# Output blocks turned on VectorE, one product and one load reordered, last forms subtracted earlier: a hybrid encoder layer on one core

## The chip, the cores and the metric

The kernel runs on one core of one Trainium2 chip. The metric is the device time of one launch in microseconds (us). The engines are TensorE (PE, with its weight loads as PEld), VectorE (DVE), ScalarE (ACT), GpSimd (POOL) and SyncE (SP), which issues most of the DMA transfers. Each engine runs its own queue of instructions in order; semaphores make one wait for another.

## The reference

One layer, for 512 prompt frames and 64 sample frames (576 columns together). All data are float32.

```python
hn = rmsnorm(x, g_norm1)
q, k, v, gb, gc, hc = split(hn @ w_in)             # 8 heads x 128 each; 1024 conv channels each
q, k = rmsnorm(q, g_q), rmsnorm(k, g_k)            # per head
o_attn = stick_breaking(q, [k_past, k], [v_past, v])   # strictly causal; the sample has 512 cached frames
u = gc * hc
o_conv = gb * (conv_w[0]*u[t-2] + conv_w[1]*u[t-1] + conv_w[2]*u[t])
x = x + concat(rmsnorm(o_attn, g_attn_out), rmsnorm(o_conv, g_conv_out)) @ w_out
h2 = rmsnorm(x, g_norm2)
x = x + (silu(h2 @ w_gate) * (h2 @ w_up)) @ w_down     # D_MODEL 2048, D_FF 5632
```

Outputs are the new x of prompt and sample, the new keys and values, and the convolution's state.

## The kernel before, in words

Activations lie with channels on the 128 partitions and the 576 frames along the free axis, in two halves of 288. A float32 product is made of three matmuls of a rounded format (fp32r): a number is split into a rounded high part and the rest, and high x high, low x high and high x low are added in PSUM. The splits cost a ScalarE cast (L228, the high part) and a VectorE subtraction (L229, the rest).

The big weight products are done by a seven-product scheme (Strassen-Winograd) on 2 x 2 blocks: two neighbouring channel tiles of the input, two of the output, two halves of the frames. One *unit* is a pair of output tiles (256 output channels) over `m` pairs of input tiles. It has seven products, numbered 1 to 7; each is `m` x 3 matmuls (`multiply`, L405) and its weights are one of seven sums of the unit's four weight blocks, made by VectorE in `weight_sums` (four additions, L345 to L353) and split into a tile `whl` by `prepare`. There are four `whl` buffers, and `prepare` runs four products ahead of `run`. The products land in three kinds of PSUM tiles: `psy` and `psv` from a rotation of three banks (`ps_pj`), `psx` (bank z0) and `psw` (bank z1 or z2 by the unit's parity). ScalarE copies partial results out (`kept`, L428), VectorE and GpSimd add them up (L445 to L452).

`order` is the hand-written list of (unit, product). It starts with `opening`; from the third unit on it repeats one pattern: the next unit's product 1, this one's 3 and 4, the next one's 2, 6, 7, 5. PE's order is always the program's. The other engines' order is made by the tile framework's scheduler in most phases; from the last unit of the gate and up phase on (`manual`), ScalarE, VectorE, SyncE and GpSimd follow the program too. A `Pipeline` of generators spaces small jobs in *ticks*: one tick is one step of `multiply`, three matmuls, and `yield 9` means nine ticks later.

Phases in order of time: input projection (to about 575 us), attention beside the output projection (to 755), second norm, gate and up (860 to 1830), down (to the end).

*Attention.* `heads` starts a head every 29 ticks; `attend` yields between its steps, with output projection products between them. At its end a head reads the sample's values with `os_` (L1296): four blocks of cached values and `vtok[:, 4]`, weighted by `ws` (an exponential on ScalarE, L1224). Then `fetch_v(h + 1)` loads the next head's values: `vtok[:, :4]` (L1045, the 512 prompt frames), `vtok[:, 4]` (L1046, the last 128 frames, sample included) and the cached `cV` (L1047); `split_v` casts the first three blocks into `hbe` and `vz`.

*Gate and up.* `finish` scales each result by the norm's row `R2`, multiplies gate and up, and `put_forms` makes the seven sums of the hidden activations (forms) for the down phase and writes them to `hid_dram` (`put_form`: cast L228, subtraction L229, DMA L1453). For the last pair `last_forms` does this in spaced steps, in the first products of the down phase.

*Down.* The order of units is the list `DOWN`; eight pairs of output tiles (`d`) are summed in SBUF blocks `acc[d, c, i]` (128 channels x 288 frames). Units 29 to 36 of the list are the last visits of each `d`: as each of their four blocks is finished, `store_y` turns it into rows of frames. Nine ticks later PE transposes the block in three pieces into PSUM (L1612), ScalarE copies it back in two instructions (L1615, L1617), and SyncE stores it (L1603, L1605, L1620), two to four DMAs a block. All 32 blocks go this way, 28 of the first seven units and four of the last, the last unit's with some of the stores on the queues of ScalarE and GpSimd. The next but one unit's weights are loaded by SyncE (L328) when a unit's products 3 and 4 have been split.

The kernel already has another way of turning a tile, in `tokens` (L807 to L815): VectorE transposes 32 x 32 blocks, and stores of 32 partitions with runs of 32 floats put them in place.

Of the kernel before, what the change touches and what calls it, by code (L numbers as in the profile page):

```python
# [10 lines left out]
F32 = mybir.dt.float32  # L11
# [5 lines left out]
P = 128  # L17
TP = 512
TS = 64
T = TP + TS  # L20
HALF = T // 2
HALVES = ((0, HALF), (HALF, T))
BK = 32
# [79 lines left out]
def tile_hybrid_stream_step(  # L103
# [6 lines left out]
    nc = tc.nc  # L110
# [5 lines left out]
    yp, ys = y_prompt[0], y_sample[0]  # L116
# [19 lines left out]
    v_dram = tc.dram_tile([NH, T, P], F32, name="v_dram")  # L136
# [4 lines left out]
    def misc(name):  # L141
        return ps_z.tile([P, 512], F32, tag="misc", name=name, bufs=2)
# [8 lines left out]
    UNITS = {n - NA: (kind, i, 0, NP) for n, (kind, i) in enumerate(HEADS_A)}  # L151
# [4 lines left out]
    NU = len(gu)  # L156
# [61 lines left out]
    pipe = Pipeline()  # L218
# [8 lines left out]
    def split(hi, lo, src, lo_eng=None):  # L227
        cast = nc.scalar.copy(out=hi, in_=src)  # L228
        (lo_eng or nc.vector).tensor_tensor(out=lo, in0=src, in1=hi.bitcast(F32), op=ALU.subtract)  # L229
        return cast.ins  # L230
# [11 lines left out]
    rows = {}  # L242
# [72 lines left out]
    def load_columns(gone=(), one=False):  # L315

        free.extend(gone)
        while wanted and room(*wanted[0]) and (one or not hold):
            n, c = wanted.pop(0)
            one = False  # L320
            src, wide_, m = source(n, c)
            halves = room(n, c)
            for h in halves:
                free.remove(h)
            t = raw_tile[halves[0][0]]
            t = t[:, halves[0][1], :] if len(halves) == 1 else t.rearrange("p h e -> p (h e)")
            t = t[:, : 2 * m * wide_]
            nc.sync.dma_start(out=t.rearrange("p (k e) -> p k e", e=wide_), in_=src)  # L328
            if c is None:
                v = t.rearrange("p (j s h c) -> p j s h c", s=2, h=2, c=P)  # L330
                region[n, 0], region[n, 1] = (v[:, :, :, 0, :], halves), (v[:, :, :, 1, :], ())
            else:
                region[n, c] = t.rearrange("p (j s c) -> p j s c", s=2, c=P), halves
# [24 lines left out]
    def prepare(n, p_):  # L358

        st = unit.setdefault(n, {"summed": -1, "split": set()})  # L360
        m = UNITS[n][3]
        if p_ == 1:
            st["a11"], st["a12"] = (region[n, 0][0][:, :, q, :] for q in range(2))
        if p_ == 6:
            while st["summed"] not in (6, 3):
                one_sum(n)
        if p_ == 3:
            while st["summed"] != 3:
                one_sum(n)
        src = {1: "a11", 2: "a12", 3: "a12", 4: "a22", 5: "s1", 6: "a11", 7: "a21"}[p_]  # L370
        slot_turn[0] += 1
        whl = wpool.tile([P, 2, NP, P], F32R, tag=("whi", "wlo")[slot_turn[0] % 2], name="whl")[:, :, :m]
        split(whl[:, 0], whl[:, 1], st[src])
        operand[n, p_] = whl
        st["split"].add(p_)
        if n >= NGU:

            if p_ == 1:
                summing.append(n)
            if summing and p_ != 2:  # L380
                k = summing[0]
                if unit[k]["summed"] != 6 or p_ == 6:
                    one_sum(k)
                if unit[k]["summed"] == 3:
                    summing.pop(0)
            if p_ in (3, 4):
                st["gone"] = st.get("gone", 0) + 1
                if st["gone"] == 2:
                    load_columns(region.pop((n, 0))[1])
            return  # L390
        for c, need in enumerate(({1, 2, 6, 3}, {5, 7, 4})):
            if p_ in need and need <= st["split"]:
                load_columns(region.pop((n, c))[1])

    def one_sum(n):
        st = unit[n]
        if "sums" not in st:
            st["sums"] = weight_sums(n)
        st["summed"] = next(st["sums"]) or 0
# [22 lines left out]
    def run(n, p_, early=False):  # L422
# [8 lines left out]
        def done(c, i, ps, part=None):  # L431
            if n < 0:
                a_finish(n, c, i, ps, part)
            elif kind != "down":
                finish(kind, fp, c, i, ps, part)
            elif n in last:
                store_y(n, c, i)
# [195 lines left out]
    with tc.manual_schedule(engines={mybir.EngineType.Activation, mybir.EngineType.DVE, mybir.EngineType.SP}):  # L633
# [60 lines left out]
        for kt in range(KD + LAG):  # L694
# [22 lines left out]
            if kt in (7, 11, 17):  # L717
                j = (kt - 7) // 4
# [255 lines left out]
    for E, h, lag in ((e1[0], 2, 8), (e1[1], 3, 22), (e0[0], 0, 36), (e0[1], 1, 50)):  # L974
# [4 lines left out]
    opening = [(0, 1), (0, 2), (1, 1), (0, 3), (0, 6), (1, 2), (0, 5), (0, 7), (1, 3), (0, 4), (1, 6), (2, 1), (1, 5),  # L979
               (1, 7), (2, 2), (1, 4), (2, 6), (2, 7), (2, 5)]  # L980
    order = [(n - NA, p_) for n, p_ in opening]
# [10 lines left out]
    for k_ in range(2, 4):  # L992
        prepare(*order[k_])
    for k_, (n, p_) in enumerate(order):
# [15 lines left out]
        if (n, p_) == (-1, 7):  # L1010
            first = next_weight(), ps_pj.tile([P, HALF], F32, tag="pj", name="pjo")
# [14 lines left out]
    vtok = bpool.tile([P, 5, P], F32, name="vtok")  # L1026
# [15 lines left out]
        nc.sync.dma_start(out=cK, in_=ck[:, h, :].rearrange("(i p) d -> p i d", p=P))  # L1042

    def fetch_v(h):
        nc.sync.dma_start(out=vtok[:, :4], in_=v_dram[h][:TP].rearrange("(i p) d -> p i d", p=P))  # L1045
        nc.sync.dma_start(out=vtok[:, 4], in_=v_dram[h][T - P :])  # L1046
        nc.sync.dma_start(out=cV, in_=cv[:, h, :].rearrange("(i p) d -> p i d", p=P))  # L1047

    load_qk(0)
# [31 lines left out]
    for h in range(NH):  # L1081
        t = tpool.tile([P, 2, T], F32R, tag=f"t{h}", name=f"mixa{h}")
# [81 lines left out]
    def attend(h):  # L1164
# [135 lines left out]
        if h + 1 < NH:  # L1300
            fetch_v(h + 1)
            split_v()
# [43 lines left out]
    down = {}  # L1346
# [101 lines left out]
    def put_form(fp, n, src):  # L1448

        t = tmp.tile([P, 2, HALF], F32R, tag="hl", name="form")  # L1450
        split(t[:, 0], t[:, 1], src)
        q = nc.gpsimd if fp == NFP - 1 else nc.sync
        q.dma_start(out=hid_dram[fp][2 * n - 2 : 2 * n].rearrange("f p t -> p f t"), in_=t.bitcast(F32))  # L1453
# [26 lines left out]
    def last_forms(s10):  # L1480
        fp, h, tt = NFP - 1, hid.pop(NFP - 1), nc.vector.tensor_tensor
        s00, s01, s11 = h[0, 0], h[0, 1], h[1, 1]
        yield 34
        tt(out=s01, in0=s01, in1=gates.pop((0, 1)), op=ALU.mult)
        yield 5
        tt(out=s10, in0=s10, in1=R2[:, :HALF], op=ALU.mult)
        tt(out=s10, in0=s10, in1=gates.pop((1, 0)), op=ALU.mult)
        for n, out, a, b in ((2, s10, None, None), (5, s00, s01, s00), (7, s01, s01, s11), (6, s11, s11, s00),
                             (4, s10, s10, s11)):
            yield 10  # L1490
            if a is not None:
                tt(out=out, in0=a, in1=b, op=ALU.subtract)
            put_form(fp, n, out)

    def finish(kind, fp, c, i, ps, part=None):
# [23 lines left out]

    slots = {}  # L1520

    order = [(0, 1), (0, 2), (1, 1), (0, 3), (0, 6), (1, 2), (0, 7), (0, 5)] + opening[8:]
    early = {0, 1}
    for n in range(2, NU):
        if n == NGU - 2:
# [13 lines left out]
    first, last = {v[0] for v in visits.values()}, {v[-1] for v in visits.values()}  # L1539

    residual = {}
    for d, v in visits.items():
        n = next(a for a, b in zip(v, v[1:]) if a >= NGU + 10 and b >= a + 4)
        residual.setdefault(n + 1, []).append(d)
    acc = {}
# [32 lines left out]
    def load_pair(p):  # L1578
# [11 lines left out]
        slots[p] = [t[:, 2 * f : 2 * f + 2, :] for f in range(FORMS)]  # L1590
        nc.sync.dma_start(out=t.bitcast(F32), in_=hid_dram[p].rearrange("f p t -> p f t"))

    def store_y(n, c, i):

        d = UNITS[n][1]
        src, cs, f0 = acc[d, c, i], slice((2 * d + c) * P, (2 * d + c + 1) * P), HALVES[i][0]
        r = HALF - 2 * P

        def put(f, ap, queue=nc.sync):

            rows, n_p = ap.shape[0], max(min(TP - f, ap.shape[0]), 0)
            if n_p:
                queue.dma_start(out=yp[f : f + n_p, cs], in_=ap[:n_p])  # L1603
            if n_p < rows:
                queue.dma_start(out=ys[f + n_p - TP : f + rows - TP, cs], in_=ap[n_p:])  # L1605

        def work():
            yield 9
            po = misc("pot")[:, : 3 * P]
            for q in range(3):  # L1610
                w = min(P, HALF - q * P)
                nc.tensor.transpose(po[:w, q * P : (q + 1) * P], src[:, q * P : q * P + w], ident)  # L1612
            yield 3
            ob = src[:, : 2 * P].rearrange("p (i c) -> p i c", c=P)
            nc.scalar.copy(out=ob, in_=po[:, : 2 * P].rearrange("p (i c) -> p i c", c=P))  # L1615
            obs = down["pool"].tile([r, P], F32, tag="obs", name="obs", bufs=4)
            nc.scalar.copy(out=obs, in_=po[:r, 2 * P :])  # L1617
            yield 4
            if i == 0:
                nc.sync.dma_start(out=yp[: 2 * P, cs].rearrange("(i p) c -> p i c", p=P), in_=ob)  # L1620
            else:
                put(f0, ob[:, 0, :])
                put(f0 + P, ob[:, 1, :], nc.scalar if n == NU - 1 else nc.sync)
            put(f0 + 2 * P, obs, nc.gpsimd if n == NU - 1 else nc.sync)

        pipe.spawn(work())


# [80 lines left out]
```

## Time and profile before

| what | value |
|---|---|
| median of 3 runs | 2344.0 us (2343.83 to 2346.86) |
| profiled execution | 2342.05 us, its span 2340.3 us |
| PE busy | 2325.7 us, 99% of the span |
| VectorE, ScalarE, GpSimd busy | 1944.2, 1232.1, 299.1 us |
| mean granted clock of TensorE | 0.999 |

Busy time of PE is a union of recorded durations, and matmuls overlap; the start-to-start distance of matmuls is what one costs. An idle gap is shown in brackets behind an instruction, with what ended it. In the window rows the columns are the stretch, its length, busy time and count of each engine that has any, the granted clock, the DMA engines' share and GB/s.

### The profile page before, as it was taken

Reading aid. Unit: us, or ns where it says so; the run is one execution under the profiler, and the core shown is the slowest. Engines: PE = TensorE matmul, PEld = TensorE weight load, DVE = VectorE, ACT = ScalarE, POOL = GpSimd, SP = SyncE. Lnnn points to the kernel's source line nnn. Section 1 sums busy time; section 2 is a strip of 40 time slices with the busy share of each in tenths; the row PEclk is TensorE's granted clock in tenths of the full one; section 3 lists DMA queues with packets and bytes.
Section 4 is the critical chain, followed back from the end, with each engine's and each line's share of the span. In section 5 each row is a group of like instructions: output and inputs, shape, how many; then the busy total and the mean of one; then the engine's idle time right before and its main releaser. Section 6 shows DMA issues by size and latency. Waiting matters only on the chain. (4 is left out here: it accounts for less than half of the span.)

```text
span 2340.3 us, 43746 instructions
## 1 busy us (share of the span) xinstructions
PE 2325.7 (99%) x17516; PEld 2317.1 (99%) x17516; DVE 1944.2 (83%) x2843; ACT 1232.1 (53%) x2226; POOL 299.1 (13%) x374
## 2 busy tenths in 40 slices
PE   9999999999999999999999999999999999999999
PEld 8999999999999999999999999999999999999998
DVE  8888989897767898888888888888887778887875
ACT  8566655455877654444444444444444444444454
POOL 0211121110432320000000000000000002431211
PEclk9999999999999999999999999999999999999999
DMA  8444344546643454553444444444444936885542
GB/s 271 136 117 129 97 135 118 135 134 207 203 129 121 169 181 128 157 159 114 154 150 127 154 137 140 152 130 149 142 139 150 347 117 227 232 217 187 198 131 82
DMA packets 509020, 368.60 MB, mean 157 GB/s; under 512 B 37462, under 2 KB 493264, under 8 KB 508816
## 3 DMA queue, kind: packets, MB, share of 16 engines
q1 hardware_dynamic: 502000, 356.32, 48.2%
q0 software_dynamic: 6384, 9.21, 2.2%
q8 instruction: 137, 2.24, 0.4%
q14 instruction: 67, 0.55, 0.1%
q10 hardware_dynamic: 432, 0.27, 0.0%
HBM read 285.52 MB, written 80.23 MB: 156 GB/s over the span
## 5 line engine op out<-in xcount | busy, mean ns | idle before, releaser
L229 DVE TENSOR_TENSOR whl<-raw_a,whl 128x1024 fp32r<-128x1024 f32 (+4 forms) x384 | 433.7, 1130 | 59.7 <-ACT whl L228 58.1
L405 PE MATMUL psy<-t,whl 128*128 128x288 f32 x3000 | 449.7, 295 | 0.0
L228 ACT CAST whl<-raw_a 128x1024 fp32r<-128x1024 f32 (+4 forms) x384 | 360.0, 939 | 135.8 <-PE psx L405 48.1
L405 PE MATMUL psy<-h_s,whl 128*128 128x288 f32 x2766 | 417.4, 295 | 1.3 <-ACT part L428 1.3
L405 PEld LDWEIGHTS psy<-t,whl 128*128 128x128 f32 x3000 | 414.7, 188 | 0.2
L405 PE MATMUL psw<-t,whl 128*128 128x288 f32 x2688 | 390.2, 295 | 0.0
L405 PEld LDWEIGHTS psy<-h_s,whl 128*128 128x128 f32 x2766 | 383.7, 188 | 1.9 <-ACT part L428 1.8
L405 PEld LDWEIGHTS psw<-t,whl 128*128 128x128 f32 x2688 | 367.0, 188 | 0.2
L229 DVE TENSOR_TENSOR whl<-raw_b,whl 128x1024 fp32r<-128x1024 f32 (+5 forms) x234 | 257.4, 1100 | 80.2 <-ACT whl L228 79.1
L228 ACT CAST whl<-raw_b 128x1024 fp32r<-128x1024 f32 (+5 forms) x234 | 211.2, 904 | 213.3 <-issue 75.2
L428 ACT COPY part<-psy 128x288 f32<-128x288 f32 x309 | 122.8, 397 | 342.3 <-PE psy L405 341.2
L405 PE MATMUL psx<-h_s,whl 128*128 128x288 f32 x1164 | 170.9, 295 | 0.0
L228 ACT CAST whl<-s 128x1024 fp32r<-128x1024 f32 (+5 forms) x103 | 95.3, 925 | 123.4 <-PE psw L405 115.3
L405 PEld LDWEIGHTS psx<-h_s,whl 128*128 128x128 f32 x1164 | 159.8, 188 | 0.0
L405 PE MATMUL psw<-t34a,whl 128*128 128x288 f32 x1056 | 150.6, 295 | 0.0
L405 PE MATMUL psy<-t12a,whl 128*128 128x288 f32 x1056 | 150.4, 295 | 0.0
L405 PEld LDWEIGHTS psy<-t12a,whl 128*128 128x128 f32 x1056 | 143.5, 188 | 0.2
L405 PEld LDWEIGHTS psw<-t34a,whl 128*128 128x128 f32 x1056 | 143.3, 188 | 0.0
L1453 POOL DMA_DIRECT2D hid_dram<-form x7 | 5.2, 737 | 954.7 <-DVE form L229 946.5
L229 DVE TENSOR_TENSOR whl<-s,whl 128x1024 fp32r<-128x1024 f32 (+5 forms) x103 | 109.9, 1067 | 20.3 <-ACT whl L228 19.6
L224 PE MATMUL pjo<-mixc,whi 128*128 128x288 f32 x512 | 120.0, 302 | 0.0
L224 PE MATMUL pjo<-mixa,whi 128*128 128x288 f32 x512 | 102.8, 295 | 0.0
(564 smaller groups left out, 3940.4 us busy)
## 6 DMA issues: line engine op xcount, KB each, us to landing
hid_dram<-form SPq DMA_DIRECT2D x147, 288.0 KB
raw_a<-in_w_in_dram SPq DMA_DIRECT2D x22, 1024.0 KB
raw_b<-in_w_in_dram SPq DMA_DIRECT2D x22, 1024.0 KB
raw_b<-in_w_gate_dram SPq DMA_DIRECT2D x22, 1024.0 KB
raw_b<-in_w_up_dram SPq DMA_DIRECT2D x22, 1024.0 KB
raw_a<-in_w_gate_dram SPq DMA_DIRECT2D x22, 1024.0 KB
raw_a<-in_w_up_dram SPq DMA_DIRECT2D x22, 1024.0 KB
h_s<-hid_dram SPq DMA_DIRECT2D x10, 2016.0 KB
```

The lines of the kernel that those rows point to most:

```text
L224: mm(ps, w_[:, k, csl], x_[:, a:b], start=(k == 0 and n == 0), stop=(k == nk - 1 and n == 2))
L228: cast = nc.scalar.copy(out=hi, in_=src)
L229: (lo_eng or nc.vector).tensor_tensor(out=lo, in0=src, in1=hi.bitcast(F32), op=ALU.subtract)
L405: mm(ps, whl[:, w_, j, :], x_, start=(start and j == 0 and q == 0), stop=(j == len(xs_) - 1 and q == 2), skip_group_check=True)
L428: nc.scalar.copy(out=t, in_=st["y"])
L1453: q.dma_start(out=hid_dram[fp][2 * n - 2 : 2 * n].rearrange("f p t -> p f t"), in_=t.bitcast(F32))
```

## The change

Four edits.

1. `store_y` hands the blocks of all units but the last to a new function `store_blocks`: nine ticks later VectorE transposes the block (32 x 32 pieces) into a spare tile, five ticks later SyncE stores it with four DMAs of 32 partitions (runs of 32 floats), and two more for the sample rows of a second half. The block just read becomes a spare tile. The last unit's blocks go through PE as before; their small copy uses halves of the spare tiles.
2. `fetch_v` loads `vtok[:, 4]` first, and `vtok[:, :4]` is issued after it.
3. `order`: (1, 7) is moved ahead of (1, 3), and `prepare` makes sure that the sums product 7 needs are there.
4. `last_forms` does each subtraction after 6 of the 10 ticks and the cast after the other 4.

```diff
@@ prepare
-        if p_ == 6:
+        if p_ in (6, 7):
             while st["summed"] not in (6, 3):
                 one_sum(n)
@@ fetch_v
-        nc.sync.dma_start(out=vtok[:, :4], in_=v_dram[h][:TP].rearrange("(i p) d -> p i d", p=P))
-        nc.sync.dma_start(out=vtok[:, 4], in_=v_dram[h][T - P :])
+        first = nc.sync.dma_start(out=vtok[:, 4], in_=v_dram[h][T - P :])
+        with tc.issue_after(first.ins):
+            nc.sync.dma_start(out=vtok[:, :4], in_=v_dram[h][:TP].rearrange("(i p) d -> p i d", p=P))
@@ last_forms
-            yield 10
+            yield 6
             if a is not None:
                 tt(out=out, in0=a, in1=b, op=ALU.subtract)
+            yield 4
             put_form(fp, n, out)
@@ order
-    order = [(0, 1), (0, 2), (1, 1), (0, 3), (0, 6), (1, 2), (0, 7), (0, 5)] + opening[8:]
+    order = [(0, 1), (0, 2), (1, 1), (0, 3), (0, 6), (1, 2), (0, 7), (0, 5), (1, 7)] + [x for x in opening[8:] if x != (1, 7)]
@@ new, ahead of store_y
+    spare = []
+
+    def store_blocks(n, c, i):
+        d = UNITS[n][1]
+        src, c0, f0 = acc[d, c, i], (2 * d + c) * P, HALVES[i][0]
+        n_p = min(HALF, TP - f0)
+
+        def work():
+            yield 9
+            if not spare:
+                spare.extend(down["pool"].tile([P, HALF], F32, tag=f"ob{k}", name="ob") for k in range(2))
+            ob = spare.pop(0)
+            nc.vector.transpose(out=ob, in_=src)
+            spare.append(src)
+            yield 5
+            for k in range(P // BK):
+                rows = ob[k * BK : (k + 1) * BK, :n_p].rearrange("j (t c) -> j t c", c=BK)
+                cg = slice(c0 + k * BK, c0 + (k + 1) * BK)
+                nc.sync.dma_start(out=yp[f0 : f0 + n_p, cg].rearrange("(t j) c -> j t c", j=BK), in_=rows)
+            for a in range(n_p, HALF, BK):
+                nc.sync.dma_start(out=ys[a - n_p : a - n_p + BK, c0 : c0 + P].rearrange("j (g c) -> g j c", c=BK),
+                                  in_=ob[:, a : a + BK])
+
+        pipe.spawn(work())
@@ store_y
+        if n < NU - 1:
+            store_blocks(n, c, i)
+            return
...
-            obs = down["pool"].tile([r, P], F32, tag="obs", name="obs", bufs=4)
+            if len(rests) % 2 == 0:
+                rests.append(spare.pop(0))
+            else:
+                rests.append(rests[-1])
+            obs = rests[-1][:r, : P] if len(rests) % 2 else rests[-1][:r, P : 2 * P]
```

More of the change, by code (lines that the diff above doesn't have):

```diff
@@ L1591, in load_pair @@
         nc.sync.dma_start(out=t.bitcast(F32), in_=hid_dram[p].rearrange("f p t -> p f t"))
+    spare = []
[19 more added lines that the diff above has]
+        pipe.spawn(work())
+    rests = []
     def store_y(n, c, i):
+        if n < NU - 1:
+            store_blocks(n, c, i)
+            return
         d = UNITS[n][1]
```

## The prediction

> **What bounds the kernel now.** I read the page first, then the stretches of time, then the timeline around every place where TensorE (PE) has a gap, and SyncE's queue last.
>
> ```profile
> span 2340.3 us, 43746 instructions
> PE 2325.7 (99%) x17516; PEld 2317.1 (99%) x17516; DVE 1944.2 (83%) x2843; ACT 1232.1 (53%) x2226; POOL 299.1 (13%) x374
> ...
> PE psy L405 11%; PE psw L405 6%; PE psx L405 3%; PE pot L1612 0%; DVE raw_a L351 0%; DVE whl L229 0%; POOL out_dram L1605 0%; POOLq L1705 0%; POOL out_dram L1603 0%; ACT obs L1617 0%; ACT acc L1615 0%; DVEq L229 0%; POOLq L1605 0%; ACTq L1603 0%; ACTq L1615 0%
> ```
>
> PE is the bound: busy 99%, and the chain is its products. So time comes off in two ways: fewer PE instructions, or the gaps that hide in the remaining 14.6 us (2340.3 less 2325.7) and in a lowered clock. The change touches one of the first kind and three of the second.
>
> **Part 1, the output blocks of the down phase.** Twenty-eight of 32 blocks lose three PE transposes, two ScalarE copies and their PSUM bank; each gains one VectorE transpose of 128x288 and more, smaller stores. The price of three transposes is not their recorded duration, because matmuls overlap; it is read from the period of a unit. Columns: stretch, length, busy time (and count) by engine.
>
> ```profile
> 1900.00:1950.00 50.00, 50.00 (x380) 50.00 (x379) 1.00 0.44 144
> ...
> 2240.77:2256.09 15.32, 15.32 (x119) 15.27 (x118) 10.99 (x16) 7.65 (x18) 2.42 (x3) 1.00 0.43 125
> ...
> sum 45.82, PE 45.82 PEld 45.67 DVE 33.08 ACT 23.06 POOL 7.39; mean PE 15.27 PEld 15.22 DVE 11.03 ACT 7.69 POOL 2.46
> ```
>
> The first row holds products alone: 380 matmuls touch 50 us, two of them at the edges, so one costs 50/378 = 0.1323 us. The last two are the first of three units of five pairs in the store stage and their sum: 7 x 15 = 105 matmuls and four blocks take 15.27 us. The matmuls are 105 x 0.1323 = 13.89; a block's transposes cost (15.27 - 13.89)/4 = 0.345 us. Twenty-eight: **-9.66 us, if VectorE and SyncE keep up.**
>
> ```profile
> L807 DVE STREAM_TRANSPOSE tok<-E-20_1697 x1: 770/770/770, 160.1 to 160.1; 128x576 f32<-128x576 f32 x1
> L807 DVE STREAM_TRANSPOSE tok<-E-5_5510 x1: 764/764/764, 499.6 to 499.6; 128x576 f32<-128x576 f32 x1
> 2249.28 0.46 DVE L450 TENSOR_TENSOR acc_z<-psx,acc_z 128x288 f32<-128x288 f32 x1 [0.35 <-PE psx L405]
> 2250.04 1.33 DVE L229 TENSOR_TENSOR whl<-raw_b,whl 128x640 fp32r<-128x640 f32 x1 [0.30 <-ACT whl L228]
> 2256.09 0.95 PE L405 MATMUL psy<-t,whl 128*128 128x288 f32 x6
> 2254.75 0.83 DVE L229 TENSOR_TENSOR whl<-raw_a,whl 128x640 fp32r<-128x640 f32 x1
> 2249.88 0.81 POOL L452 TENSOR_TENSOR acc_z<-acc_z,part 128x288 f32<-128x288 f32 x1 [7.63 <-DVE acc_z L450]
> 2217.24 0.92 PE L405 MATMUL psx<-t,whl 128*128 128x288 f32 x5 [0.25 <-DVE whl L229]
> 2228.25 1.75 DVE L229 TENSOR_TENSOR whl<-raw_b,whl 128x640 fp32r<-128x640 f32 x2
> 2234.01 0.79 PE L405 MATMUL psy<-t,whl 128*128 128x288 f32 x4
> ```
>
> VectorE: the first and last of nine transposes of twice the width took 0.77 us; half is 0.385, the lower bound. An add of the same 128x288 took 0.46. The upper bound is that add stretched as the split at 2250.04 is (1.33 beside the GpSimd add at 2249.88, against 0.83 at 2254.75): 0.46 x 1.33/0.83 = 0.74. I take 0.45, nearest to the add. Per unit VectorE goes from 11.03 busy to 12.8, of 13.89: 92%. What covers it is lead: that split ended at 2251.37 and PE took it up at 2256.09, 4.7 us later. The thin place is the start of the stage: at 2217.24 PE had just waited for a split, so the lead was nothing; by 2234.01 it is 4.0 (that split ended at 2228.25 + 1.75 = 2230.00). In these 17 us the change puts three transposes on VectorE (1.35) and takes three sets off PE (1.0), which leaves 1.6 of the 4.0. I book +0.5 us for waits of single splits, bounds 0 and +4.0, the whole lead.
>
> Behind a transpose on VectorE stand the next split and add; the transpose itself waits for GpSimd's last addition into the block, which by the queue order is one product older, so I book nothing for that wait; without that cover it costs one GpSimd add, 0.81 us, out of the lead.
>
> ```profile
> L812 SPq DMA_DIRECT2D out_dram<-tok x36: 345/593/1812, 161.9 to 501.9; - x36
> L815 SPq DMA_DIRECT2D out_dram<-tok x18: 536/589/1284, 164.4 to 503.2; - x18
> 2240.34 0.40 SPq L328 DMA_DIRECT2D raw_b<-in_w_down_dram  x1
> 2249.28 0.73 ACT L228 CAST whl<-raw_b 128x640 fp32r<-128x640 f32 x1 [1.21 <-PE psx L405]
> ```
>
> SyncE: a block now needs four stores (first half) or six, 20 per unit against 12. The kernel already has such 32-row stores; their median issue is 0.59 us, so 20 x 0.59 + 0.40 for the weight load = 12.2 us of 13.89. Ahead of each weight load stand ten of these stores, 5.9 us, the first ready about when the second product after its block ends; I put the load 1 us later than now. It has 8.9 us today from issue to first cast (2240.34 to 2249.28), less 1.4 for the shorter period. What is late then is ScalarE's cast, by under 1 us, inside the lead of 4.7. I book +0.2. At the very end the last unit still goes through PE, and its stores follow ten of the new ones (5.9 us) that start some 8 us earlier: 0.
>
> The page DMA: Bandwidth & Descriptors of the Trainium skill (Rules for kernel authors) speaks against this part: coalesce small transfers, under 64 KB one pays mostly overhead. That is rival C below; no row here shows it binding in this stage.
>
> **Part 2, the value loads of attention.** The load of the first four value blocks is put behind the load of the fifth, which must wait until the sample matmuls (L1296) have read the old one. Columns: start, duration, instruction, idle before.
>
> ```profile
> 639.54 0.37 SPq L1045 DMA_DIRECT2D vtok<-v_dram  x1
> 648.29 0.30 ACT L228 CAST vz<-vtok 128x128 fp32r<-128x128 f32 x1 [4.53 <-DMA vtok<-v_dram]
> 648.50 0.43 ACT L1224 ACTIVATE ws<-zs 128x320 f32<-128x320 f32 x1
> 648.98 1.10 PE L1296 MATMUL zs<-ws,cV 128*128 128x64 f32 x8 [2.29 <-ACT ws L1224]
> 650.58 0.46 SPq L1046 DMA_DIRECT2D vtok<-v_dram  x1
> 664.14 0.38 PE L1279 MATMUL po<-pr,vtok 128*128 128x128 f32 x2
> 648.00:652.00 4.00, 3.02 (x23) 3.02 (x23) 2.32 (x6) 3.53 (x9) 0.65 (x2) 0.89 0.19 50
> 652.00:656.00 4.00, 4.00 (x23) 4.00 (x23) 1.63 (x4) 2.87 (x8) 1.76 (x3) 0.68 0.59 180
> ACT vz L228 <- DMA vtok<-v_dram: 6.8, 4, 4.5
> ```
>
> Today the early load lets the next head's cast of the values stand ahead of this head's exponential in ScalarE's queue. Once the load took 8.7 us; ScalarE sat 4.53 us, PE 2.29, and the granted clock was 0.89 and 0.68 in the next 8 us, worth 4 x 0.11 + 4 x 0.32 = 1.7 us. After the change the cast cannot stand there, since its data waits for matmuls that need that exponential. Gone: 2.29 + 1.7 = **-4.0 us**. Next late: the same cast behind the later load. The loads go from 639.54 to about 651 in this head, and PE needs them only in the next head's value product at 664.14, 13 us on; but ScalarE waits in order, and the four waits of today sum to 6.8 us. I book +0.5, bounds 0 and +4.0 (the same stall elsewhere).
>
> The Trainium skill (TensorE: Matmul & The Clock Gate, What's actually happening) has the clock fall after an idle window of about 3.4 us. By that, a stall of 2.29 us would have cost no clock and this part would be worth 1.8 instead of 3.5; the rows show the clock falling, so the rows stand.
>
> **Part 3, seventh product earlier; part 4, last forms.** Columns as before.
>
> ```profile
> 879.91 0.39 ACT L428 COPY part<-psy 128x288 f32<-128x288 f32 x1
> 880.35 0.43 PEld L405 LDWEIGHTS psv<-h_z,whl 128*128 128x128 f32 x3 [0.73 <-ACT part L428]
> 876.33 1.22 DVE L229 TENSOR_TENSOR whl<-raw_b,whl 128x1024 fp32r<-128x1024 f32 x1
> 1858.71 0.95 DVE L345 TENSOR_TENSOR s<-raw_a 128x768 f32<-128x768 f32 x1
> 1859.58 0.45 DVE L1492 TENSOR_TENSOR ut<-ux,ut 128x288 f32<-128x288 f32 x1
> 1860.07 0.43 ACT L228 CAST form<-ut 128x288 fp32r<-128x288 f32 x1 [2.26 <-DVE ut L1492]
> 1860.85 1.06 PE L405 MATMUL psy<-h_s,whl 128*128 128x288 f32 x6 [0.85 <-ACT part L428]
> 1865.16 0.43 ACT L228 CAST form<-ux 128x288 fp32r<-128x288 f32 x1 [3.11 <-DVE ux L1492]
> 1865.94 1.06 PE L405 MATMUL psy<-h_s,whl 128*128 128x288 f32 x6 [0.46 <-ACT part L428]
> ```
>
> Part 3: the second unit's third product needs a bank that the copy at 879.91 frees, and PE's next weight load waits 0.73. The seventh writes another bank, so it runs over the copy. Its split needs three sums instead of four: it can be ready about when the split at 876.33 was, 2 us ahead of need. I book **-0.6** (0 to -0.73). The extra condition on the sums adds no instruction.
>
> Part 4: ScalarE's cast waits for a subtraction that VectorE reaches late (L345 stands before it), and a PSUM copy behind the cast holds PE 0.85 and 0.46 us. Four ticks earlier is 4 x 3 x 0.1323 = 1.6 us of queue, which takes the subtraction ahead of L345 (0.95). I book **-1.2** (0 to -1.31); the weight split behind it slips 0.45 us, inside its lead.
>
> **Sum.** The profiled execution took 2342.05 us (its span 2340.3 and 1.75 around it); the median shown is 2344.0, 1.95 more. -9.66 + 0.5 + 0.2 - 4.0 + 0.5 - 0.6 - 1.2 = -14.3 us: 2327.8 against 2342.05, **2329.7** against the median. A measurement can tell about 0.2% (4.7 us).
>
> **The rivals.** *B, the attention stall only moves.* For it: ScalarE is in order, and big weight loads still go out near the new places. Against: the 13 us of time. Part 2 gives 0 instead of -3.5: 2333.2, up to 2337 with the start of the store stage at its bound. *C, SyncE becomes the bound of the store stage.* At 0.72 us an issue (single ones reach 1.8) a unit needs 20 x 0.72 + 0.4 = 14.8 us, 0.9 more than PE's 13.89; seven units give back 6.3: 2336.0. It decides above 0.67 us an issue. *D, slower: VectorE in series.* Today it idles 15.27 - 11.03 = 4.24 us a unit, the largest part of it for ScalarE's casts (the row below: who waited, for whom, sum, times and longest, 2219 to 2334). If all of that stays and the transposes come on top, a unit takes 15.27 + 1.8 instead of 13.89: seven units are 12.6 slower than now, less 5.3 of the other parts: 2351.3. It decides where the lead of 4.7 us is used up. Against it: casts run ahead while VectorE is late, so idle time fills first.
>
> ```profile
> DVE whl L229 <- ACT whl L228: 20.9, 35, 1.4
> ```
>
> *E, the gain is eaten in small waits* of each of these kinds: no change, about 2342.
>
> **How the numbers follow.** Forecast 0.55 (2325 to 2333); B 0.16; C 0.13; E 0.08; D 0.08. Faster 0.55 + 0.16 + 0.13 = 0.84, same 0.08, slower 0.08. The range leaves out D and E: from 2325 (all gains at their bounds give 2344.0 - 9.66 - 4.0 - 0.73 - 1.31 = 2328.3, and the three runs shown differ by 3 us) to 2338.
>
> **What would show it.** Right: twelve transposes at L1612's successor instead of 96; unit periods of 13.9 us; no PE wait on the exponential, and clock 1.00 between 640 and 660; no wait on the part copy at 880, 1860 and 1865. Wrong: PE waiting on splits after 2217, SyncE without a pause in the last 100 us, ScalarE waiting for the value load elsewhere, or a lowered clock in another head.

## The result, and the profile after

| kernel | time, median (lowest to highest) | against before on the same chip, 95% |
|---|---|---|
| before | 2345.49 us (2343.68 to 2347.94), 7 runs | |
| after | 2339.02 us (2337.46 to 2339.39), 7 runs | 0.9973 [0.9963, 0.9983] |

The change makes the kernel 6.5 us faster; 14.3 were forecast, and 2339.0 lies 1.0 us above the range. The profiled execution after took 2339.12 us. Its page, the first two lines and TensorE's row of the 40 slices:

```profile
span 2337.4 us, 43553 instructions
PE 2316.1 (99%) x17432; PEld 2306.9 (99%) x17432; DVE 1954.1 (84%) x2871; ACT 1221.6 (52%) x2170; POOL 300.6 (13%) x374
...
PE   9999999999999999999999999999999999999997
```

TensorE has 84 instructions fewer (28 blocks of three transposes) and 9.6 us less busy time, yet the span fell by only 2.9. The 7 in the last slice (a 9 before) says where to look: the end. I lined up PE's instructions of the two traces and took the length of each stage.

| stage, in the profiles | before | after | step | forecast |
|---|---|---|---|---|
| attention, first score matmul to the first product of its own output projection | 169.57 | 169.25 | -0.3 | -3.5 |
| second gate unit's seventh product | | | -0.76 | -0.6 |
| last forms | | | -1.85 | -1.2 |
| store stage, last 820 weight products | 118.99 | 109.14 | -9.85 | -8.96 |
| tail, last weight product to the end | 6.78 | 14.74 | +7.96 | 0 |

The steps sum to -4.8. The 1.9 us that are missing to -2.9 are waits of other places that come and go between executions of the same instructions. Two waits of the first phase (from 174 us on, for a ScalarE copy and a VectorE subtraction) cost 1.7 us after and nothing before; shorter waits ahead of them give back 0.7, and one wait at 1991 us costs 0.9. The two of the first phase are there in the kernel with edit 1 alone too, whose first phase has the code of before, and of a1 and c2 below, which are one kernel, only a1's profile has them.

The store stage, in windows (columns as before), the transposes by line (least, median and longest ns), and everything that PE waited for in the whole span (sum, times, longest):

```profile
2239.98:2253.86 13.88, 13.88 (x107) 13.88 (x106) 12.84 (x20) 6.10 (x10) 3.13 (x4) 1.00 0.57 138
...
2239.98:2282.02 42.04, 42.04 (x320) 42.04 (x319) 38.66 (x58) 18.33 (x30) 9.24 (x10) 1.00 0.59 144
```

```profile
L1607 DVE STREAM_TRANSPOSE acc<-acc x14: 464/467/474, 2273.5 to 2318.2; 128x288 f32<-128x288 f32 x14
```

```profile
PE psx L556 <- DMA xin<-in_x_prompt_dram: 4.0, 2, 3.7
PE zs L1220 <- DVE spl L229: 1.6, 4, 0.6
PE psy L405 <- ACT part L428: 1.0, 2, 0.6
PE ss L284 <- DVE s L905: 0.7, 1, 0.7
PE pot L1644 <- ACT acc L1653: 0.3, 1, 0.3
PE zs L1219 <- ACT sph L228: 0.3, 1, 0.3
PE psx L405 <- DVE whl L229: 0.3, 1, 0.3
```

A unit takes 13.88 us, VectorE is busy 12.84 of it, a transpose takes 0.467, and PE waits for a weight split once, 0.3 us. The wait on the exponential (2.3 us before) is gone from the list, but four waits on `spl` have come, the low part of the split behind the sample columns' weights (the samples' split, in what follows). Of these waits only the 0.3 us of `pot` lies in the tail. What makes the tail long is read in SyncE's queue: its timeline (start, time to the end of the row's last instruction, line, count) and its waits after 2300.

```profile
2308.44 18.29 SPq L1613 DMA_DIRECT2D out_dram<-acc  x12
2326.78 1.13 SPq L1615 DMA_DIRECT2D out_dram<-acc  x2
2328.01 1.97 SPq L1613 DMA_DIRECT2D out_dram<-acc  x4
...
2334.76 0.42 SPq L1635 DMA_DIRECT2D out_dram<-acc  x1
```

```profile
SPq L1613 <- DMA out_dram<-acc: 11.2, 2, 11.0
SPq L1613 <- DVE acc L450: 5.6, 4, 1.9
```

Twelve stores took 18.29 us: one of them waited 11.0 us, for a *transfer of results*, not for data and not for a slow issue. In those 11 us (2314.4 to 2325.4) the DMA engines were nearly idle, as these two windows show (last columns: DMA share, GB/s):

```profile
2315.00:2320.00 5.00, 5.00 (x40) 4.99 (x40) 3.10 (x7) 1.40 (x4) 2.04 (x2) 1.00 0.03 5
2320.00:2325.00 5.00, 4.18 (x32) 3.61 (x30) 0.92 (x2) 1.51 (x7) 1.83 (x3) 1.00 0.05 13
```

The transfer is the last unit's own: ScalarE issues it when PE and ScalarE have turned the last unit's block.

```profile
2323.67 0.25 ACT L1653 COPY acc<-pot 32x128 f32<-32x128 f32 x1
2323.80 0.34 ACTq L1635 DMA_DIRECT2D out_dram<-acc  x1
```

The instruction lists of the compiled kernel tell what the two stores have in common. In this kernel each DMA of SyncE and of ScalarE signals one of eight completion counts (`DMAHW0` to `DMAHW7`, handed out in turn to both) and waits until the count's last holder has landed:

```
SyncE    753 L1613 DMA out<-acc5 32x9x32   waits DMAHW3
         754 L1613 DMA out<-acc5 32x9x32   waits DMAHW5
         755 L1613 DMA out<-acc5 32x9x32   waits DMAHW7
         756 L1613 DMA out<-acc5 32x9x32   waits DMAHW1
         757 L1613 DMA out<-acc5 32x7x32   waits DMAHW3
         758 L1613 DMA out<-acc5 32x7x32   waits DMAHW4
ScalarE 2097 L1635 DMA out<-acc4 96x128    waits DMAHW4
        2098 L1637 DMA out<-acc4 32x128    waits DMAHW6
...
        2103 L1635 DMA out<-acc4 96x128    waits DMAHW0
        2104 L1637 DMA out<-acc4 32x128    waits DMAHW2
```

SyncE skips 4, 6, 0 and 2: these went to ScalarE's four stores. So SyncE's row 758, whose data had long been ready, waits for count 4, which ScalarE's store holds from 2323.80 to 2325.41 (its landings in the trace); SyncE goes on at 2325.43 and needs until 2335.2 for the rest. The semaphores in the trace say the same: SyncE's and ScalarE's stores signal the same eight in turn, GpSimd's stores eight others, and the store at 2325.43 waits for the one that the store at 2323.80 signals. In the kernel before, ScalarE's first late store comes behind all but two of SyncE's in the order in which the counts are handed out.

### The profile page after: what moved, and what is told of

It is laid out like the page before. It is cut to its first block, busy times and chain, and to the rows that moved or that the text cites. A ratio compares the mean times of both kernels' runs of the same rounds, so it can differ in the third digit from the quotient of the medians.

```text
span 2337.4 us, 43553 instructions
## 1 busy us (share of the span) xinstructions
PE 2316.1 (99%) x17432; PEld 2306.9 (99%) x17432; DVE 1954.1 (84%) x2871; ACT 1221.6 (52%) x2170; POOL 300.6 (13%) x374
## 4 chain that ended last, share of the span: by engine, by line
PE 92%; DVE 3%; ACT 3%; DMA 1%; issue 1%; POOL 0%; SPq 0%; POOLq 0%; DVEq 0%; ACTq 0%
PE psy L405 45%; PE psw L405 23%; PE psx L405 11%; PE pjo L224 6%; PE pj L691 1%; PE pjz L691 1%; DVE whl L229 1%; PE psv L405 1%; PE pjm L691 1%; DMA raw_a<-in_w_down_dram 0%; ACT ph L228 0%; PE psx L556 0%; ACT whi L176 0%; DMA raw_b<-in_w_down_dram 0%; PE z L1176 0%
```

## The experiments

All were timed in five rounds; those of one letter ran on one chip with the kernel before.

| kernel | time | against before, 95% | attention | store | tail |
|---|---|---|---|---|---|
| a1 last unit's store on SyncE | 2330.37 | 0.9936 [0.9923, 0.9948] | 169.66 | 109.17 | 6.49 |
| a2 without edit 1 | 2340.81 | 0.9983 [0.9974, 0.9992] | 170.10 | 119.00 | 6.80 |
| a3 without edit 2 | 2340.36 | 0.9981 [0.9972, 0.9989] | 170.32 | 109.11 | 14.86 |
| a4 edit 1 alone | 2343.41 | 0.9992 [0.9983, 1.0001] | 171.73 | 109.16 | 14.65 |
| b1 a1, old order, block 4 doubled | 2331.46 | 0.9941 [0.9928, 0.9955] | 171.37 | 109.18 | 6.50 |
| b2 a1 without edit 2 | 2332.67 | 0.9949 [0.9936, 0.9961] | 172.02 | 109.15 | 6.49 |
| b3 that store on GpSimd | 2331.26 | 0.9945 [0.9932, 0.9957] | 169.30 | 109.20 | 7.56 |
| c1 a1, value rows early | 2326.79 | 0.9923 [0.9909, 0.9937] | 166.14 | 109.20 | 6.49 |
| c2 a1 again | 2330.36 | 0.9941 [0.9928, 0.9953] | 169.82 | 109.22 | 6.50 |
| c3 edit 2 alone | 2343.23 | 0.9994 [0.9985, 1.0003] | 168.87 | 119.01 | 6.78 |

Before had medians of 2344.99 (a), 2344.86 (b) and 2344.29 us (c). The last three columns are stage lengths (us) in each kernel's one profile.

**a1: is the tail the shared count?**

```diff
-                put(f0 + P, ob[:, 1, :], nc.scalar if n == NU - 1 else nc.sync)
+                put(f0 + P, ob[:, 1, :], nc.sync)
```

> The changed kernel with the last unit's two stores that went out on ScalarE's queue put on SyncE's queue. Theory T1: the tail is long because a SyncE store of the last unit but one waits 11 us (2314.4 to 2325.4) for a completion count that only ScalarE's store at 2323.80 delivers. Then the wait goes with that store, SyncE issues its stores without a pause, the stretch from PE's last product to the end falls from 14.6 to 7 to 8 us, and the time from 2339.0 to 2331 to 2333 us. Rival T2: SyncE cannot issue 140 small stores in time. Then two more stores on SyncE make it no better: 2339 to 2340 us.

It measured 2330.37, a little below the 2331 to 2333 of theory T1 and 8.6 us less than after, by the name of a queue alone. SyncE's timeline:

```profile
2309.70 7.46 SPq L1613 DMA_DIRECT2D out_dram<-acc  x12
2317.21 1.13 SPq L1615 DMA_DIRECT2D out_dram<-acc  x2
2318.44 1.88 SPq L1613 DMA_DIRECT2D out_dram<-acc  x4
...
2327.91 0.42 SPq L1637 DMA_DIRECT2D out_dram<-acc  x1
```

Twelve stores take 7.46 us where they took 18.29, the last one goes out at 2327.91, and the tail is 6.49 us, about that of before (6.78).

**b3: is it any other queue, or the shared counts?** GpSimd's DMAs take no `DMAHW` count.

```diff
-                put(f0 + P, ob[:, 1, :], nc.scalar if n == NU - 1 else nc.sync)
+                put(f0 + P, ob[:, 1, :], nc.gpsimd if n == NU - 1 else nc.sync)
```

> The changed kernel with the last unit's store of ScalarE's queue put on GpSimd's queue instead. Theory T1 (the 11 us in which SyncE issued nothing are a wait for a completion count that ScalarE's store holds, and SyncE's and ScalarE's stores share their counts): GpSimd's stores are of another kind of queue with counts of their own, so SyncE issues its stores without a gap from 2309 on, and the time is 2329.5 to 2332. Rival T2 (any store of the last unit outside SyncE's queue holds SyncE up, because counts are handed out over all queues or SyncE waits for the last unit's data): the gap of some 11 us stays and the time is 2338 to 2340.

```profile
2309.21 7.46 SPq L1613 DMA_DIRECT2D out_dram<-acc  x12
2316.72 1.13 SPq L1615 DMA_DIRECT2D out_dram<-acc  x2
```

There is no gap, though the store stands outside SyncE's queue as in the changed kernel: theory T1 holds and T2 is out. The tail is 1.1 us longer than a1's, as GpSimd issues all its stores in a row to the very end.

**a2 and a4: the stores and the rest apart.** a2 leaves `store_y` as in the kernel before; a4 is the kernel before with edit 1 alone (the condition `p_ in (6, 7)` of edit 3 stays and does nothing there).

```diff
 a2, against after
     def store_y(n, c, i):
-        if n < NU - 1:
-            store_blocks(n, c, i)
-            return
...
 a4, against before
     def store_y(n, c, i):
+        if n < NU - 1:
+            store_blocks(n, c, i)
+            return
```

> The changed kernel with the store edit undone (all 32 blocks through PE); the other three edits stay. By the two traces the other edits are worth about 3 us: first forms 1.85, gate 0.76, attention 0.3; so 2342 to 2343 us against 2345.5 before. Rival: the profile of before caught a mild run of the attention stall, the other edits are worth 5 to 6 us, and the store edit is worth little: 2339.5 to 2340.5 us.

> The kernel before with the store edit alone. By the traces the store stage gains 9.8 us and the tail gives back 7.9: about 2343 to 2344 us against 2345.5. Rival: the edits add up otherwise (the tail's loss needs the other edits' timing): 2336 us if the tail stays at 6.6 us.

Edits 2 to 4 are worth 4.2 us (2344.99 - 2340.81; 5.3 forecast). That is more than the 3 us or so expected from the two traces: a2 came out 1.2 us below its range, toward its rival, since edit 2 is worth more than those two profiles show (below). Edit 1 alone is worth 1.6 us (8.96 forecast), and a4's interval includes a ratio of 1. a4's profile has the store stage at 109.16 and the tail at 14.65: ten gained, eight given back. With a1's tail, edit 1 is worth 2340.81 - 2330.37 = 10.4 us.

**a3, b2 and c3: edit 2 apart.** a3 and b2 undo it in after and in a1; c3 has it alone.

```diff
 a3 and b2
-        first = nc.sync.dma_start(out=vtok[:, 4], in_=v_dram[h][T - P :])
-        with tc.issue_after(first.ins):
-            nc.sync.dma_start(out=vtok[:, :4], in_=v_dram[h][:TP].rearrange("(i p) d -> p i d", p=P))
+        nc.sync.dma_start(out=vtok[:, :4], in_=v_dram[h][:TP].rearrange("(i p) d -> p i d", p=P))
+        nc.sync.dma_start(out=vtok[:, 4], in_=v_dram[h][T - P :])
```

> The changed kernel with the value loads of attention in the old order. Theory: the stall of 4.0 us only moved into four waits of 0.4 to 0.7 us on the sample's split, so the old order costs 0 to 1.5 us more: 2339 to 2340.5 us, with the exponential behind the value cast again. Rival: the new order saves the whole 4 us in most runs: 2343 us.

> The changed kernel with the last unit's store on SyncE's queue, and the value rows loaded as in the kernel before (edit 2 undone). The waits of 0.3 to 0.6 us on the samples' split go and the one of 2.3 us on the exponential comes back. If edit 2 is worth 1.3 us as the pair with the late store said: 2331.2 to 2332.2. If the two waits are worth the same: 2329.9 to 2330.9. If edit 2 is worth its forecast of 3.5: 2333.4 to 2334.4.

> The kernel before with edit 2 alone (value rows: block 4 first, blocks 0 to 3 behind it). By the stage lengths of the profiles so far (with the old load 169.6 to 172.0 us, mean 171.0; with the new 169.3 to 170.1, mean 169.6): 1.4 us less than the kernel before, 2343.0 to 2344.2 where that has 2345.0. By the forecast's own term (3.5): 2341.0 to 2342.0. If the stall only moves at its whole price: 2344.6 to 2345.4.

Edit 2 measures 1.1 us (c3 against before), 1.3 (after's 2339.02 against a3, not timed together) and 2.3 (a1 against b2, different chips); b2's time falls between what was expected for 1.3 and for 3.5. No single one of these is much more than its uncertainty, but all have one sign, and the stage lengths agree: old load 169.6 to 172.0, mean 171.0 in five profiles; new load 168.9 to 170.1, mean 169.5 in six. So about 1.5 us, not 3.5 and not 0.

**b1 and c1: why not 3.5?** In the trace of after, the two casts of the next head's values (`hbe`, `vz`) and their subtractions now run ahead of the next head's scores. ScalarE's casts, then VectorE, then PE, all of after:

```profile
655.88 0.40 ACT L228 CAST hbe<-vtok 128x256 fp32r<-128x256 f32 x1
656.18 0.29 ACT L228 CAST vz<-vtok 128x128 fp32r<-128x128 f32 x1
```

```profile
656.74 0.45 DVE L229 TENSOR_TENSOR hbe<-vtok,hbe 128x256 fp32r<-128x256 f32 x1
657.12 0.41 DVE L229 TENSOR_TENSOR vz<-vtok,vz 128x128 fp32r<-128x128 f32 x1
657.45 0.62 DVE L1229 SCALAR_TENSOR_TENSOR z<-z,mneg 128x128 f32<-128x128 f32 x2
...
664.17 0.75 DVE L229 TENSOR_TENSOR spl<-hbl,sph 128x576 fp32r<-128x576 f32 x1
```

```profile
664.09 0.30 PE L1219 MATMUL zs<-sph,trir 128*128 128x320 f32 x1
664.98 0.42 PE L1220 MATMUL zs<-spl,trir 128*128 128x320 f32 x1 [0.58 <-DVE spl L229]
```

The mask of the scores starts at 657.45, behind the two subtractions, and from there the chain runs to the samples' split, which ends at 664.92 where PE wanted it at 664.23. Two kernels test this. b1 goes back to the old order of the loads but gives block 4 a buffer pair, so that its load waits for nothing:

```diff
+        lastv.append(bpool.tile([P, P], F32, tag="v4", name="v4", bufs=2))
         nc.sync.dma_start(out=vtok[:, :4], in_=v_dram[h][:TP].rearrange("(i p) d -> p i d", p=P))
-        nc.sync.dma_start(out=vtok[:, 4], in_=v_dram[h][T - P :])
+        nc.sync.dma_start(out=lastv[-1], in_=v_dram[h][T - P :])
```

> The changed kernel with the last unit's store on SyncE's queue (2330.4 us so far), and the value rows loaded in the order of the kernel before (blocks 0 to 3 first), but block 4 in a buffer of its own, of which there are two, so that its load waits for no product. Theory W (edit 2 gave back its gain because all five blocks now wait for the last product of the head before, so that the two casts run some 9 us later on ScalarE and push the splits late): here neither the exponential waits nor the splits; the wait of 2.3 us on the exponential is gone, the four waits of 0.3 to 0.6 us on the samples' split too, the attention stage takes 166.5 to 168.5 us instead of 169.7, and the time is 2326.5 to 2329.0. Rival M (ScalarE is full there, the delay comes out somewhere in the stage whatever the order of the loads): the stage stays at 169.3 to 170.5, the time at 2329.8 to 2331.5.

That missed: b1 takes 2331.46, and the old stall is back. The wait of PE and the windows around it:

```profile
PE zs L1298 <- ACT ws L1226: 2.2, 1, 2.2
```

```profile
648.00:652.00 4.00, 1.81 (x12) 1.66 (x12) 1.09 (x3) 2.17 (x7) 0.46 (x1) 0.91 0.05 11
652.00:656.00 4.00, 4.00 (x19) 4.00 (x19) 2.62 (x5) 3.45 (x9) 1.41 (x3) 0.50 0.52 145
656.00:660.00 4.00, 4.00 (x25) 4.00 (x24) 2.20 (x5) 3.12 (x8) 1.26 (x3) 0.74 0.26 84
```

Block 4 was not the point: the load that the cast waits for (blocks 0 to 3) still goes out at 640.5, in the busiest stretch of the DMA engines. So the theory held only in part, and I gave c1 the other half: the three blocks that are cast get a tile pair of their own and are loaded right behind the cached keys, while the casts keep about their old places.

```diff
+    def fetch_v3(h):
+        v3.append(bpool.tile([P, 3, P], F32, tag="v3", name="v3", bufs=2))
+        nc.sync.dma_start(out=v3[-1], in_=v_dram[h][: 3 * P].rearrange("(i p) d -> p i d", p=P))
...
             load_cached_keys(h + 1)
+            fetch_v3(h + 1)
```

> The changed kernel with the last unit's store on SyncE's queue, and the value rows that are cast (blocks 0 to 2) in a tile of their own, of which there are two, loaded a head's third earlier, right behind the cached keys; blocks 3 and 4 as in the kernel before. ScalarE's order keeps the two casts where the kernel before has them. Theory W (the 2.3 us wait came from the load, and the waits on the samples' split from the casts' later place; neither is left): the stage of attention takes 166.0 to 168.5 us in the profile, with no wait above 0.5 us, and the time is 2326.5 to 2329.3. Rival M (ScalarE and VectorE are the limit there and the time comes out as other waits): the stage takes 169.0 to 170.5 us, the time is 2329.8 to 2331.5.

> The changed kernel with the last unit's store on SyncE's queue again, beside the kernel with the value rows early on one chip: 2329.5 to 2331.5 by its first runs (2330.4); the attention stage 169.3 to 170.1 us in the profile.

c1 measures 2326.79 and c2, the same but for the value rows, 2330.36: 3.6 us, and the stage is 166.14 us, 3.4 less than the mean of the new load. SyncE, ScalarE, VectorE and PE of c1, at the two places shown of after:

```profile
630.66 0.38 SPq L1047 DMA_DIRECT2D v<-v_dram  x1
```

```profile
643.26 0.28 ACT L228 CAST vz<-v 128x128 fp32r<-128x128 f32 x1
...
645.48 0.42 ACT L1231 ACTIVATE ws<-zs 128x320 f32<-128x320 f32 x1
```

```profile
656.83 0.62 DVE L1235 SCALAR_TENSOR_TENSOR z<-z,mneg 128x128 f32<-128x128 f32 x2
...
663.30 0.74 DVE L229 TENSOR_TENSOR spl<-hbl,sph 128x576 fp32r<-128x576 f32 x1
```

```profile
664.07 0.31 PE L1225 MATMUL zs<-sph,trir 128*128 128x320 f32 x1
664.21 0.31 PE L1226 MATMUL zs<-spl,trir 128*128 128x320 f32 x1
```

The load goes out at 630.66 where the kernel before sent it at 639.54, the cast finds its data, and the exponential follows at 645.48 without a stall. At the second place PE stands at the same instant in both traces (664.07 against 664.09): here the split starts at 663.30 instead of 664.17 and PE doesn't wait. Of the four waits on the samples' split one is left:

```profile
PE zs L1226 <- DVE spl L229: 0.4, 1, 0.4
```

A wait of 0.6 us on the copy of the cached keys is new, just above the 0.5 that was expected as the most. Matched one by one with c2's, c1's matmuls gain 2.8 us at the places of these splits and 0.8 at the last head's value products; the other places cancel. c1 is also the fastest version: 0.9923 of before [0.9909, 0.9937].

## Why the prediction was right or wrong

*Part 1, the store stage: right.* The forecast was -9.66 with 0.7 booked for waits; it measured -9.85, so next to nothing of the 0.7 was needed. The transpose was put at 0.45 us (0.467), VectorE at 12.8 of 13.89 (12.84 of 13.88), and the lead held: PE waited 0.3 us for a split, which was there before as well. Rivals C and D are out as stated: SyncE never held PE up, and twelve of its stores took 7.46 us in a1, 0.62 each, under the 0.67 from which C was to decide.

*Part 1, the very end: the step that failed.* "At the very end the last unit still goes through PE, and its stores follow ten of the new ones (5.9 us) that start some 8 us earlier: 0." It measured +7.96. I counted SyncE's issue time and when the blocks were ready, and looked past the change's own effect on which DMA is handed which completion count. In that order ScalarE's first late store now stands ahead of 23 of SyncE's, where it stood ahead of two. a1 (same stores, one queue) and b3 (another queue, other counts) both give the time back, so the wait and its holder are shown; why the order came out so (20 stores a unit instead of 12, so that more of them are outstanding when ScalarE's turn comes) is only argued. None of the four rivals had it: the measured 2339.0 lies between C's 2336.0 and E's 2342, but SyncE's issue rate was not the bound (C), and the gains were there and one large wait took them back, not many small ones (E).

*Part 2, attention: right about what goes, wrong about what is late next.* This is the second step that failed, and the smaller one. The stall and the lowered clock are gone: in the trace of after every window from 640 to 660 has the clock at 1.00, among them the two in which it was 0.89 and 0.68.

```profile
648.00:652.00 4.00, 4.00 (x34) 3.92 (x33) 2.29 (x4) 3.00 (x8) 1.25 (x3) 1.00 0.30 83
652.00:656.00 4.00, 4.00 (x33) 4.00 (x33) 2.44 (x5) 3.80 (x10) 2.15 (x5) 1.00 0.61 212
```

But the place of the stall was taken by waits on the samples' split; with edit 2 worth 1.5, the booked "+0.5, bounds 0 and +4.0" should have been about +2.5. I looked for the next late thing where ScalarE waits for the load, and it was the 0.7 us of VectorE that the two casts bring with them, put ahead of a chain with almost no slack (in c1, without them there, the split ends at 664.04 and PE wants it at 664.21). Rival B, "the attention stall only moves", was in large part right. The profile that the forecast was made from had a stage of 169.57 us, and c1's is 3.43 shorter: -3.5 is what this part is worth against that profile when, of both kinds of wait, next to nothing is left; against the old load's mean of 171.0 it is 4.9.

The price of the stall was also undersized in the profile that I read: there it cost 1.7 us of clock, while in b1's rows above the clock fell to 0.91, 0.50 and 0.74, worth 4 x (0.09 + 0.50 + 0.26) = 3.4 us. Finer windows show what differs: the clock is at 0.50 for one stretch of 3.4 us in the profile before (651.1 to 654.5) and in a3's, and for one of 6.8 us in a4's, b1's (651.3 to 658.1) and b2's. The profile before had the shortest attention stage of the five with the old load, so its own time was no fair base for this part.

The rule of the Trainium skill (TensorE: Matmul & The Clock Gate, What's actually happening), an idle window of about 3.4 us, does not agree with these rows: b1's clock fell after PE had waited 2.2 us. The measurement decides.

*Parts 3 and 4: right.* -0.76 against -0.6 and -1.85 against -1.2, the same in every kernel that has them. The last forms gained more than the bound of 1.31 (0.85 + 0.46), because the idle times in brackets understate the two waits: from start to start PE's products came 1.0 and 0.6 us late, and the first six behind each wait took 0.1 us longer (1.06 against 0.95). Both waits are gone after: from 1858 to 1867 PE runs without a gap.

*The base.* The sum was set against a median of 2344.0, and before's medians were 2344.3 to 2345.5. By the steps of the table, with edit 2 at -1.5: -1.5 - 0.76 - 1.85 - 9.85 + 7.96 = -6.0 us, against 6.5 measured.

## What to carry to other kernels

When a change adds DMAs to one queue, look at what they share with the DMAs of other queues: completion counts handed out in turn can make a ready transfer wait for one that is issued much later, and a single late store on another queue is enough. In the profile such a wait shows as a queue that waits for a *DMA* of results while the DMA engines are idle. And where a wait goes because work was put elsewhere, follow that work to its new place on every engine it touches, and judge the stage from several executions before its stall is priced.

## What the runs showed of the hardware

The granted clock after one and the same stall differed between profiles: after about 2.3 us without products it was 0.89 and 0.68 in the next windows of the profile before, and 0.91, 0.50 and 0.74 in b1's, that is, one stretch of 3.4 us at 0.50 or one of 6.8. A stall of that size can cost more in clock (3.4 us in b1) than in idle time (2.2).

One load of 0.25 MB issued at 639.54 landed 8.7 us later in the profile before, when the DMA engines' share in the 4 us windows around it was 1.04 and 0.72; in c1 the load of the three blocks, issued at 630.66 ahead of that stretch, held up no cast of ScalarE's (the first ran at 643.26).
